# Transformer block on one core: three more matrix sections in seven products, two of the block sums added by DMA, one more raw buffer

## The chip, the cores and the metric

The kernel runs on one core of one Trainium2 chip. The metric is device microseconds of one execution, the median of several; lower is better. The engines are TensorE (PE; weight loads are listed as PEld), VectorE (DVE), ScalarE (ACT), GpSimd (POOL) and SyncE (SP), which here only issues DMAs. GpSimd can issue DMAs too.

## The reference

One layer of a hybrid block on x of 256 rows by 1024 columns, float32: a feed-forward with half weight, a token mixer, a second feed-forward. All projections take 1024 columns in; the feed-forwards go to 4096 and back.

```python
x = x + 0.5 * rmsnorm(swiglu(rmsnorm(x, pre1), w_gate, w_up, w_down), post1)
h = rmsnorm(x, mix_pre)
q, k, v, f, u, sv, ga, gb = split(h @ w_in)                  # 1024 each, f: 8
o_a = forgetting_attention(q, k, v, f)                       # 8 heads of 128, causal
o_b = gelu(u) * (w_s @ layernorm(gelu(sv)) + b_s)            # in groups of 128 columns
x = x + rmsnorm((sigmoid(ga) * o_a + sigmoid(gb) * o_b) @ w_out, mix_post)
x = x + 0.5 * rmsnorm(swiglu(rmsnorm(x, pre2), w_gate2, w_up2, w_down2), post2)
# swiglu(h, g, u, d) = (silu(h @ g) * (h @ u)) @ d
```

## The kernel before, in words

**Precision.** Every float32 operand is split into a high part (ScalarE, a cast, line 86) and a low part (VectorE, the difference, line 87), and every product is three matmuls: high by high, high by low, low by high. A weight quarter is 128 x 2048 floats, 1 MB: four blocks of 128 rows by 512 columns. It is loaded by SP into one of five `raws` buffers, split into a pair of `hi` and `lo` in one of four `wts` pairs, and then used by TensorE. A pair is free again when its last matmul has ended, and a raw buffer when both parts (and sums from it) are made.

**Sections.** A projection of 1024 by 1024 columns is a "section". The ordinary form (`section`, `section_by_tile`, line 223) takes the four quarters in turn and each serves both row tiles: 8 steps of 12 matmuls of 512 columns. The form in seven products (`fast`, line 298) is a Winograd scheme on 2 x 2 blocks: the activations in quarters, of which four sums (`parts`) are made once by `sums`, and the weights in quarters b11, b12, b22, b21, of which sums are made on the way. Each of seven products P1 to P7 is again 12 matmuls, with a split of its own for its weight (a quarter or a sum of quarters), and VectorE mixes the results (`u2`, `w`, `y11`, `y01`, `y10`, line 306). The weight sums are adds in the raw buffers (line 302). Before, this form is used for `up` of blocks 1 to 3 of both feed-forwards.

**Feed-forward.** `ffn` goes through four blocks of 1024 hidden columns: gate, then up, then the gated result is transposed (`hp`, `hT`). Between the steps of block b stand the down steps (`y`, line 363) of block b - 1, two groups of 12 matmuls from each down quarter (`d`). Block 0 has none, the last block's come at the end.

**Mixer.** v, then attention head by head, each with two half-heads of 16 matmul pairs; scores, transposes and values are put off by a few steps (`later`). Then sv with its LayerNorm, u, ga, gb and the output projection.

**Order.** Each engine runs its own instructions in the order of the program, which the scheduler of the building layer fixes; a wait holds up all that stands behind it on that engine. SP's loads are one queue; a load waits for its raw buffer. Norm gains are loaded into two buffers of their own (`gains`).

The lines that choose the form and hold the sums:

```python
FAST1 = {(b, "u") for b in range(1, NB)}
FAST2 = {(b, "u") for b in range(1, NB)}
FASTM = set()
...
    raws = ctx.enter_context(tc.tile_pool(name="raws", bufs=5))
    wts = ctx.enter_context(tc.tile_pool(name="wts", bufs=4))
    gains = ctx.enter_context(tc.tile_pool(name="gains", bufs=2))
```

## Time and profile before

| what | value |
|---|---|
| median of 3 runs | 751.82 us (751.54 to 752.13) |
| the profiled execution | 752.29 us, of which the span of the trace is 750.5 |
| granted TensorE clock over the span | 0.993 |
| busy: TensorE, VectorE, ScalarE, GpSimd | 736.4, 544.4, 380.0, 12.9 us |
| loaded from memory | 140.02 MB, 188 GB/s over the span |

The span runs from the first to the last instruction of the trace; the rest of the profiled execution lies around it. A share of busy time is a mean over stages that differ; what bounds a stage is read in its own window.

### The profile page before, as it was taken

How to read it: one execution, taken by the hardware profiler on the slowest of the kernel's cores; microseconds unless marked ns; L12 is line 12 of the kernel's file. 1: busy time of each engine (PE TensorE's matmuls, PEld its weight loads, DVE VectorE, ACT ScalarE, POOL GpSimd, SP SyncE). 2: the span in 40 equal slices, each digit the busy share in tenths (PEclk: the TensorE clock that was granted, in tenths of full speed). 3: DMA queues.
4: the chain of work that ended last, by engine and by line, in shares of the span. 5: the costliest groups of instructions: out<-in, count | busy, mean ns of one | idle time of the engine just before them, and what ended most of it. 6: DMA issues, size and time to landing. Idle time of an engine off the chain costs nothing.

```text
span 750.5 us, 8526 instructions
## 1 busy us (share of the span) xinstructions
PE 736.4 (98%) x3446; PEld 609.0 (81%) x3446; DVE 544.4 (73%) x565; ACT 380.0 (51%) x397; POOL 12.9 (2%) x20
## 2 busy tenths in 40 slices
...
GB/s 333 335 258 231 57 225 298 149 72 342 203 57 196 336 144 187 279 169 113 161 120 281 163 117 224 145 179 265 169 56 250 307 116 104 340 172 57 224 56 57
DMA packets 22695, 141.62 MB, mean 189 GB/s; under 512 B 3264, under 2 KB 3520, under 8 KB 6528
## 3 DMA queue, kind: packets, MB, share of 16 engines
q1 hardware_dynamic: 22656, 141.08, 51.4%
...
HBM read 140.02 MB, written 1.05 MB: 188 GB/s over the span
## 4 chain that ended last, share of the span: by engine, by line
PE 91%; DVE 4%; issue 1%; POOL 1%; ACT 1%; DMA 1%; SPq 0%; POOLq 0%; DVEq 0%; ACTq 0%
PE g L223 22%; PE y L363 22%; PE u L223 9%; PE qk L202 4%; PE sv L223 3%; PE ga L223 3%; PE gb L223 3%; PE qk L203 2%; PE hp L384 2%; PE v L223 2%; PE u_3D L298 1%; PE u_1C L298 1%; PE u_2C L298 1%; PE wo L223 1%; PE u_1D L298 1%; PE u_2D L298 1%
## 5 line engine op out<-in xcount | busy, mean ns | idle before, releaser
L223 PE MATMUL g<-hi_g,xT 128*128 128x512 f32 x512 | 165.8, 395 | 0.5 <-ACT xT L86 0.5
L363 PE MATMUL y<-hi_d,hT 128*128 128x512 f32 x512 | 147.4, 391 | 0.0
L223 PEld LDWEIGHTS g<-hi_g,xT 128*128 128x128 f32 x512 | 97.3, 190 | 21.3 <-ACT xT L86 1.3
L363 PEld LDWEIGHTS y<-hi_d,hT 128*128 128x128 f32 x512 | 95.7, 188 | 19.4
L87 DVE TENSOR_TENSOR lo_g<-raw_g,hi_g 128x2048 fp32r<-128x2048 f32 (+1 forms) x50 | 74.9, 1518 | 42.0 <-ACT hi_g L86 42.0
L223 PE MATMUL g<-lo_g,xT 128*128 128x512 f32 x256 | 100.7, 393 | 1.1 <-DVE lo_g L87 1.1
L87 DVE TENSOR_TENSOR lo_d<-raw_d,hi_d 128x2048 fp32r<-128x2048 f32 x32 | 73.0, 2286 | 36.8 <-ACT hi_d L86 36.6
L363 PE MATMUL y<-lo_d,hT 128*128 128x512 f32 x256 | 80.8, 392 | 0.0
L86 ACT CAST hi_g<-raw_g 128x2048 fp32r<-128x2048 f32 (+1 forms) x50 | 62.8, 1292 | 32.9 <-PE u L223 9.3
L86 ACT CAST hi_d<-raw_d 128x2048 fp32r<-128x2048 f32 x32 | 60.8, 1914 | 25.4 <-PE g L223 8.6
L223 PE MATMUL u<-hi_u,xT 128*128 128x512 f32 x192 | 60.6, 391 | 0.0
L223 PEld LDWEIGHTS g<-lo_g,xT 128*128 128x128 f32 x256 | 48.5, 190 | 11.9 <-DVE lo_g L87 2.1
L363 PEld LDWEIGHTS y<-lo_d,hT 128*128 128x128 f32 x256 | 47.8, 188 | 9.7
L302 DVE TENSOR_TENSOR raw_u<-raw_u,raw_u 128x2048 f32<-128x2048 f32 x24 | 55.0, 2292 | 0.8
L369 ACT ACTIVATE sg<-g 128x512 f32<-128x512 f32 x32 | 18.8, 597 | 60.5 <-PE g L223 60.5
L202 PE MATMUL qk<-xT,hi_qk 128*128 128x512 f32 x128 | 46.6, 405 | 0.0
L86 ACT CAST hi_u_3p<-raw_u 128x2048 fp32r<-128x2048 f32 x14 | 26.6, 1914 | 32.9 <-DVE raw_u L302 26.0
L223 PEld LDWEIGHTS u<-hi_u,xT 128*128 128x128 f32 x192 | 36.1, 188 | 7.3
L87 DVE TENSOR_TENSOR lo_u_3p<-raw_u,hi_u_3p 128x2048 fp32r<-128x2048 f32 x14 | 31.9, 2288 | 9.4 <-ACT hi_u_3p L86 9.4
L223 PE MATMUL u<-lo_u,xT 128*128 128x512 f32 x96 | 37.4, 389 | 0.0
L86 ACT CAST hi_u_2p<-raw_u 128x2048 fp32r<-128x2048 f32 x14 | 26.8, 1917 | 20.1 <-DVE raw_u L302 9.5
L86 ACT CAST hi_u_1p<-raw_u 128x2048 fp32r<-128x2048 f32 x14 | 26.8, 1917 | 20.1 <-DVE raw_u L302 9.5
(256 smaller groups left out, 1264.7 us busy)
## 6 DMA issues: line engine op xcount, KB each, us to landing
raw_u<-in_u SPq DMA_DIRECT2D x32, 1024.0 KB, 4.8
raw_d<-in_dn SPq DMA_DIRECT2D x32, 1024.0 KB, 4.8
raw_g<-in_g SPq DMA_DIRECT2D x30, 1024.0 KB, 4.9
raw_qk<-in_w_qk SPq DMA_DIRECT2D x8, 1024.0 KB, 5.0
raw_v<-in_w_v SPq DMA_DIRECT2D x4, 1024.0 KB, 5.2
raw_sv<-in_w_sv SPq DMA_DIRECT2D x4, 1024.0 KB, 4.8
raw_u<-in_w_u SPq DMA_DIRECT2D x4, 1024.0 KB, 4.7
raw_ga<-in_w_ga SPq DMA_DIRECT2D x4, 1024.0 KB, 4.8
```

The lines of the kernel that those rows point to most:

```text
L86: return [nc.scalar.copy(out=hi, in_=src), nc.vector.tensor_tensor(out=lo, in0=src, in1=hi.bitcast(F32), op=ALU.subtract)]
L87: nc.vector.tensor_tensor(out=lo, in0=src, in1=hi.bitcast(F32), op=ALU.subtract)]
L202: nc.tensor.matmul(ps, lhsT=hi, rhs=xT[:, k], start=k == 0, stop=False, skip_group_check=True)
L203: nc.tensor.matmul(top, lhsT=lo, rhs=xT[:, k, :, 0, :], start=False, stop=k == KT - 1, skip_group_check=True)
L223: nc.tensor.matmul(ps, lhsT=xT[:, kh * 4 + k, t, xs, :], rhs=v, start=kh == 0 and k == 0 and q == 0, stop=kh == 1 and k == 3 and q == 2)
L298: nc.tensor.matmul(ps, lhsT=lhs(k, xs), rhs=z, start=start and k == 0 and q == 0, stop=k == 3 and q == 2, skip_group_check=True)
L302: nc.vector.tensor_tensor(out=out, in0=p, in1=q, op=ALU.add)
L363: nc.tensor.matmul(ys[t][c], lhsT=hTs[f // 4][:, f % 4, t, xs, :], rhs=w[:, c * 512:(c + 1) * 512], start=f == 0 and q == 0, stop=f == NF ...
L369: nc.scalar.activation(out=sg, in_=y, func=AF.Silu)
L384: nc.tensor.transpose(out=ps[:, i * P:(i + 1) * P], in_=h[:, i * P:(i + 1) * P], identity=ident)
```

## The change

**Where seven products are used.** In both feed-forwards gate of block 2 joins the three ups, and in the mixer ga. The sums of activations for the mixer (`sums("mx")`) are made during attention, ahead of head 5, and ga is moved from behind u to the place right behind attention.

**Two sums by DMA.** Where gate of a block is in the set (block 2), and for ga, `fast` gets `dma=True`. The weight sums for P5 and P7 are then not adds of VectorE: one quarter is loaded by SP, and GpSimd issues a DMA that reads the second quarter and adds it to the buffer (`accum_op`). b12 is loaded twice. The sums for P6 and P4 stay with VectorE, so each such section has two sums on each side, where the section before had four on VectorE.

**Order of products.** P1 P5 P6 P2 P3 P7 P4 in place of P1 P5 P6 P2 P7 P3 P4, in all such sections; the sum for P4 is made right behind P2.

**Buffers.** Six raw buffers in place of five; the two gain buffers are gone, and gains are loaded as pairs into a raw buffer where they are used.

```diff
-FAST1 = {(b, "u") for b in range(1, NB)}
-FAST2 = {(b, "u") for b in range(1, NB)}
-FASTM = set()
+FAST1 = {(b, "u") for b in range(1, NB)} | {(2, "g")}
+FAST2 = FAST1
+FASTM = {"ga"}
...
-    raws = ctx.enter_context(tc.tile_pool(name="raws", bufs=5))
+    raws = ctx.enter_context(tc.tile_pool(name="raws", bufs=6))
-    gains = ctx.enter_context(tc.tile_pool(name="gains", bufs=2))
...
+    def gain(*names, by=D):
+        pair = raws.tile([P, 2048], F32, tag="raw", name=f"g_{names[0]}")
+        gs = [pair[:, i * D:(i + 1) * D] for i in range(len(names))]
...
-    def fast(src, name, parts, done):
+    def fast(src, name, parts, done, dma):
...
+        def two(first, second):
+            raw = get(*first)
+            nc.gpsimd.dma_start(out=raw, in_=src[second], accum_op=ALU.add)
+            return raw
...
-        b12 = get(1, 0)
-        add(b11, b11, b12)
+        if dma:
+            t1 = two((1, 0), (0, 0))
+        else:
+            b12 = get(1, 0)
+            add(b11, b11, b12)
+            t1 = b11
         c = bank(f"{name}C")
-        product(c, lhs_s(0), b11, "p5", True)
+        product(c, lhs_s(0), t1, "p5", True)
         yield
         b22 = get(1, 1)
-        add(b11, b11, b22)
+        add(b11, t1, b22)
...
-        add(b12, b12, b22)
         b21 = get(0, 1)
         product(a, lhs_x(1, 0), b21, "p2", False)
         done(0, 0, a)
+        add(b11, b11, b21)
         yield
-        d = bank(f"{name}D")
-        product(d, lhs_s(2), b12, "p7", True)
-        done(1, 1, mixed("y11", w, d, ALU.subtract))
-        yield
+        if not dma:
+            add(b12, b12, b22)
         product(c, lhs_s(3), b22, "p3", False)
         done(0, 1, mixed("y01", c, u2, ALU.subtract))
         yield
-        add(b11, b11, b21)
+        d = bank(f"{name}D")
+        product(d, lhs_s(2), two((1, 0), (1, 1)) if dma else b12, "p7", True)
+        done(1, 1, mixed("y11", w, d, ALU.subtract))
+        yield
         product(d, lhs_x(1, 1), b11, "p4", False)
...
-                    steps.append((fast(src, nm, parts, fn), 7))
+                    steps.append((fast(src, nm, parts, fn, (b, "g") in quick), 7))
...
-            later(1, lambda: values(pT))
+            later(1 if h < 6 else 2, lambda: values(pT))
...
-        parts = [sums("mx")] if FASTM else None
+        parts = []
...
-        oA = attention(v, *kept)
+        oA = attention(v, *kept, between=lambda: parts.append(sums("mx")))
+
+        def ga_done(t, c, ps):
+            oc = oA[:, t, c * 512:(c + 1) * 512]
+            sg = mid_tile([P, 512], f"sga{t}{c}")
+            nc.scalar.activation(out=sg, in_=ps, func=AF.Sigmoid)
+            later(5, lambda: nc.vector.tensor_tensor(out=oc, in0=oc, in1=sg, op=ALU.mult))
+
+        columns(a["w_ga"], "ga", ga_done)
```

The listings of the two programs count 3382 matmuls before and 3346 now; 599 instructions of VectorE in place of 561; five weight loads more on SP and ten DMAs on GpSimd.

**What this moves.** VectorE's order in the first feed-forward, from the low part (`lo`) of up's P4 in block 1 on. The names carry the section, block and product: `u1_1p4` is P4 of up, feed-forward 1, block 1, `g1_2` gate of block 2, `d1_8` a down quarter, `sg` a gating, `hT` the low part of a transposed half. Before:

```order
L87 TENSOR_TENSOR lo_u1_1p4_883<-raw_u1_100_693,hi_u1_1p4_882 128x2048
L306 TENSOR_TENSOR u1_1y11_825<-u1_1w_774,u1_1D_808 128x512
L87 TENSOR_TENSOR lo_g1_200_925<-raw_g1_200_922,hi_g1_200_924 128x2048
L376 TENSOR_TENSOR sg1_111_679<-u1_1y11_825,sg1_111_679 128x512
L87 TENSOR_TENSOR hT1_2_828<-hp1_100_829,hT1_2_828 128x4x128
L306 TENSOR_TENSOR u1_1y01_852<-u1_1C_717,u1_1u2_772 128x512
L87 TENSOR_TENSOR lo_d1_8_962<-raw_d1_8_959,hi_d1_8_961 128x2048
L376 TENSOR_TENSOR sg1_101_677<-u1_1y01_852,sg1_101_677 128x512
L87 TENSOR_TENSOR hT1_3_855<-hp1_111_856,hT1_3_855 128x4x128
L306 TENSOR_TENSOR u1_1y10_898<-u1_1D_808,u1_1u2_772 128x512
L376 TENSOR_TENSOR sg1_110_583<-u1_1y10_898,sg1_110_583 128x512
L87 TENSOR_TENSOR lo_g1_201_980<-raw_g1_201_977,hi_g1_201_979 128x2048
```

Now:

```order
L89 TENSOR_TENSOR lo_u1_1p4_880<-raw_u1_100_690,hi_u1_1p4_879 128x2048
L309 TENSOR_TENSOR u1_1y01_822<-u1_1C_714,u1_1u2_769 128x512
L89 TENSOR_TENSOR lo_g1_2p1_921<-raw_g1_200_917,hi_g1_2p1_920 128x2048
L390 TENSOR_TENSOR sg1_101_674<-u1_1y01_822,sg1_101_674 128x512
L89 TENSOR_TENSOR hT1_2_825<-hp1_100_826,hT1_2_825 128x4x128
L309 TENSOR_TENSOR u1_1y11_850<-u1_1w_771,u1_1D_833 128x512
L89 TENSOR_TENSOR lo_g1_2p5_950<-raw_g1_210_945,hi_g1_2p5_949 128x2048
L390 TENSOR_TENSOR sg1_111_676<-u1_1y11_850,sg1_111_676 128x512
L89 TENSOR_TENSOR hT1_3_853<-hp1_101_854,hT1_3_853 128x4x128
L309 TENSOR_TENSOR u1_1y10_895<-u1_1D_833,u1_1u2_769 128x512
L305 TENSOR_TENSOR raw_g1_200_917<-raw_g1_210_945,raw_g1_211_983 128x2048
```

The low part of P5 (its raw buffer `raw_g1_210` is the one that GpSimd adds to) stands where the low part of a down quarter stood, ahead of a gating, a transposed half, a mixed sum and the sum for P6.

Further on, VectorE's order in block 2, from the low part of up's P5 to that of P2. Before:

```order
L87 TENSOR_TENSOR lo_u1_2p5_1145<-raw_u1_200_1119,hi_u1_2p5_1144 128x2048
L302 TENSOR_TENSOR raw_u1_200_1119<-raw_u1_200_1119,raw_u1_211_1178 128x2048
L87 TENSOR_TENSOR lo_d1_12_1163<-raw_d1_12_1160,hi_d1_12_1162 128x2048
L87 TENSOR_TENSOR lo_u1_2p6_1183<-raw_u1_200_1119,hi_u1_2p6_1182 128x2048
L302 TENSOR_TENSOR raw_u1_200_1119<-raw_u1_200_1119,raw_u1_201_1203 128x2048
L87 TENSOR_TENSOR lo_u1_2p2_1206<-raw_u1_201_1203,hi_u1_2p2_1205 128x2048
```

Now:

```order
L89 TENSOR_TENSOR lo_u1_2p5_1160<-raw_u1_210_1155,hi_u1_2p5_1159 128x2048
L305 TENSOR_TENSOR raw_u1_200_1134<-raw_u1_210_1155,raw_u1_211_1193 128x2048
L309 TENSOR_TENSOR g1_2y10_1118<-g1_2D_1060,g1_2u2_1003 128x512
L89 TENSOR_TENSOR lo_d1_12_1178<-raw_d1_12_1175,hi_d1_12_1177 128x2048
L89 TENSOR_TENSOR lo_u1_2p6_1198<-raw_u1_200_1134,hi_u1_2p6_1197 128x2048
L305 TENSOR_TENSOR raw_u1_200_1134<-raw_u1_200_1134,raw_u1_201_1217 128x2048
L89 TENSOR_TENSOR lo_u1_2p2_1220<-raw_u1_201_1217,hi_u1_2p2_1219 128x2048
```

The last mixed sum of gate (`y10`) and the low part of `d12` now stand behind the low part of P5 and the sum that both read its buffer.

GpSimd's order up to the norms of the first feed-forward's end. Before:

```order
L154 TENSOR_TENSOR r_f10_120<-r_f10_120,power_91 128x1
L154 TENSOR_TENSOR r_f11_130<-r_f11_130,power_91 128x1
L154 TENSOR_TENSOR r_p10_1864<-r_p10_1864,power_91 128x1
L154 TENSOR_TENSOR r_mx0_1874<-r_mx0_1874,power_91 128x1
L154 TENSOR_TENSOR r_p11_1952<-r_p11_1952,power_91 128x1
L154 TENSOR_TENSOR r_mx1_1962<-r_mx1_1962,power_91 128x1
```

Now:

```order
L156 TENSOR_TENSOR r_f10_117<-r_f10_117,power_88 128x1
L156 TENSOR_TENSOR r_f11_127<-r_f11_127,power_88 128x1
L315 DMA raw_g1_210_945<-in_g1 128x2048
L315 DMA raw_g1_210_1061<-in_g1 128x2048
L315 DMA raw_u1_210_1155<-in_u1 128x2048
L315 DMA raw_u1_210_1277<-in_u1 128x2048
L156 TENSOR_TENSOR r_p10_1880<-r_p10_1880,power_88 128x1
L156 TENSOR_TENSOR r_mx0_1890<-r_mx0_1890,power_88 128x1
L156 TENSOR_TENSOR r_p11_1968<-r_p11_1968,power_88 128x1
```

Four adding DMAs of block 2 stand between the norms at the start and those at the end. In the mixer two stand ahead of the roots for sv's LayerNorm, and in the second feed-forward again four.

SP's order from the first load of block 2's gate. Before:

```order
L102 DMA raw_g1_200_922<-in_g1 128x2048
L102 DMA raw_d1_8_959<-in_dn1 128x2048
L102 DMA raw_g1_201_977<-in_g1 128x2048
L102 DMA raw_g1_210_1025<-in_g1 128x2048
L102 DMA raw_d1_10_1055<-in_dn1 128x2048
L102 DMA raw_g1_211_1073<-in_g1 128x2048
L102 DMA raw_u1_200_1119<-in_u1 128x2048
L102 DMA raw_u1_210_1140<-in_u1 128x2048
```

Now:

```order
L104 DMA raw_g1_200_917<-in_g1 128x2048
L104 DMA raw_g1_210_945<-in_g1 128x2048
L104 DMA raw_d1_8_965<-in_dn1 128x2048
L104 DMA raw_g1_211_983<-in_g1 128x2048
L104 DMA raw_g1_201_1007<-in_g1 128x2048
L104 DMA raw_g1_210_1061<-in_g1 128x2048
L104 DMA raw_d1_10_1084<-in_dn1 128x2048
L104 DMA raw_u1_200_1134<-in_u1 128x2048
L104 DMA raw_u1_210_1155<-in_u1 128x2048
L104 DMA raw_d1_12_1175<-in_dn1 128x2048
```

`raw_g1_210` and `raw_u1_210` each stand twice: first the load for P5's sum, then, behind b21 (`201`), the second load of b12 for P7's. The load for P5's sum takes the buffer that b21 of the section before has had.

## Rows read from the trace of the kernel before

**Rows 1.** The page's parts 1 and 3: busy times, DMA queue.

```profile
PE 736.4 (98%) x3446; PEld 609.0 (81%) x3446; DVE 544.4 (73%) x565; ACT 380.0 (51%) x397; POOL 12.9 (2%) x20
...
q1 hardware_dynamic: 22656, 141.08, 51.4%
```

**Rows 2.** The chain of waits in block 2: start, length, what.

```profile
133.24 5.44 PE g L223 x24
...
160.44 2.72 PE u_2C L298 x12
163.16 2.72 PE y L363 x12
...
168.60 2.72 PE u_2A L298 x12
```

**Rows 3.** Busy time by window, block 2 and its up half.

```profile
core 0: us, PE busy (x) PEld busy (x) DVE busy (x) ACT busy (x) POOL busy (x), PEclk, DMA share, GB/s
124.60:189.10 64.50, 64.50 (x293) 53.28 (x293) 50.91 (x33) 33.51 (x24) 0.00 (x0) 1.00 0.53 197
157.70:189.10 31.40, 31.40 (x146) 25.89 (x145) 30.20 (x22) 19.27 (x13) 0.00 (x0) 1.00 0.73 267
```

**Rows 4.** Timeline of VectorE: start, length, line, operation.

```profile
117.16 0.68 DVE L87 TENSOR_TENSOR hT<-hp,hT 128x512 fp32r<-128x512 f32 x1
117.76 0.68 DVE L306 TENSOR_TENSOR u_1y<-u_1C,u_1u 128x512 f32<-128x512 f32 x1
118.36 2.28 DVE L87 TENSOR_TENSOR lo_d<-raw_d,hi_d 128x2048 fp32r<-128x2048 f32 x1
120.55 0.68 DVE L376 TENSOR_TENSOR sg<-u_1y,sg 128x512 f32<-128x512 f32 x1
...
121.76 0.68 DVE L306 TENSOR_TENSOR u_1y<-u_1D,u_1u 128x512 f32<-128x512 f32 x1
...
145.72 4.62 DVE L302 TENSOR_TENSOR raw_u<-raw_u,raw_u 128x2048 f32<-128x2048 f32 x2
150.25 2.28 DVE L87 TENSOR_TENSOR lo_u_2p<-raw_u,hi_u_2p 128x2048 fp32r<-128x2048 f32 x1
```

**Rows 5.** Busy time by window: late attention, sv (columns as in rows 3).

```profile
330.00:360.00 30.00, 30.00 (x195) 27.07 (x194) 16.76 (x31) 14.78 (x33) 0.00 (x0) 1.00 0.40 136
360.70:386.70 26.00, 26.00 (x132) 21.84 (x132) 18.43 (x52) 12.35 (x20) 2.10 (x2) 1.00 0.27 86
```

**Rows 6.** Timeline of VectorE: the same step of two heads.

```profile
344.84 0.29 DVE L527 TENSOR_REDUCE nmx<-S 128x1 f32<-128x128 f32 x1 [2.64 <-PE S L522]
...
352.44 0.29 DVE L527 TENSOR_REDUCE nmx<-S 128x1 f32<-128x128 f32 x1 [2.64 <-PE S L522]
```

**Rows 7.** DMA issues: count, KB each, median us from issue to landing.

```profile
raw_u<-in_u SPq DMA_DIRECT2D x32, 1024.0 KB, 4.8
...
g_ffn_post_g<-in_ffn_post_g SPq DMA_DIRECT2D x2, 512.0 KB, 5.5
```

**Rows 8.** The view of one tile, gate's raw buffers: landings.

```profile
DMA to landing us min/median/max: 4.7/5.4/9.0
```

**Rows 9.** Timeline of SP's queue in block 1's up.

```profile
102.08 0.33 SPq L102 DMA_DIRECT2D raw_g<-in_g  x1
```

**Rows 10.** Timeline of ScalarE: casts, idle before them and what ended it.

```profile
115.53 1.92 ACT L86 CAST hi_d<-raw_d 128x2048 fp32r<-128x2048 f32 x1 [0.82 <-PE u_1C L298]
...
121.44 1.91 ACT L86 CAST hi_g<-raw_g 128x2048 fp32r<-128x2048 f32 x1 [2.84 <-PE u_1D L298]
...
124.62 1.91 ACT L86 CAST hi_g<-raw_g 128x2048 fp32r<-128x2048 f32 x1 [0.80 <-PE y L363]
```

More of the change, by code (lines that the diff above doesn't have):

```diff
@@ L76, in block @@
     nc.vector.memset(power, -0.5)
-    def gain(name, by=D):
-        g = gains.tile([P, D], F32, tag="g", name=f"g_{name}")
-        for c in range(0, D, by):
-            nc.sync.dma_start(out=g[:, c:c + by], in_=a[name][:, c:c + by])
-        return g
+    def gain(*names, by=D):
+        pair = raws.tile([P, 2048], F32, tag="raw", name=f"g_{names[0]}")
+        gs = [pair[:, i * D:(i + 1) * D] for i in range(len(names))]
+        for name, g in zip(names, gs):
+            for c in range(0, D, by):
+                nc.sync.dma_start(out=g[:, c:c + by], in_=a[name][:, c:c + by])
+        return gs
     def split(hi, lo, src):
@@ L493, in forget_gates, with attention @@
         nc.vector.tensor_copy(out=cs[:, 2], in_=cs[:, 0].bitcast(F32))
-    def attention(v, cs, idr, pick):
+    def attention(v, cs, idr, pick, between):
         oA = big.tile([P, NT, D], F32, tag="b", name="oA")
         for h in range(H):
+            if h == 5:
+                between()
             w = quarter(a["w_qk"][h // 2, h % 2], f"qk{h}")
@@ L561, in mixer @@
         run(section_by_tile(a["w_v"], "v", v_done, 4))
-        parts = [sums("mx")] if FASTM else None
+        parts = []
         def columns(src, name, done):
-            run(fast(src, name, parts, done) if name in FASTM else section(src, name, done))
-        oA = attention(v, *kept)
+            run(fast(src, name, parts, done, True) if name in FASTM else section(src, name, done))
+        oA = attention(v, *kept, between=lambda: parts.append(sums("mx")))
[5 more added lines that the diff above has]
+        columns(a["w_ga"], "ga", ga_done)
         ws = aux.tile([P, H, P], F32, tag="aux", name="ws")
@@ L575, in mixer @@
         nc.sync.dma_start(out=bs, in_=a["b_s"])
-        lng, lnb = gain("sgu_ln_g"), gain("sgu_ln_b")
+        lng, lnb = gain("sgu_ln_g", "sgu_ln_b")
         vn = big.tile([P, NT, D], F32, tag="b", name="vn")
@@ L617, in mixer @@
         columns(a["w_u"], "u", u_done)
-        def ga_done(t, c, ps):
-            oc = oA[:, t, c * 512:(c + 1) * 512]
-            sg = mid_tile([P, 512], f"sga{t}{c}")
-            nc.scalar.activation(out=sg, in_=ps, func=AF.Sigmoid)
-            nc.vector.tensor_tensor(out=oc, in0=oc, in1=sg, op=ALU.mult)
-        columns(a["w_ga"], "ga", ga_done)
         ms = {}
@@ L642, in mixer @@
         run(section_by_tile(a["w_gb"], "gb", gb_done))
-        gp, gn = gain("mix_post_g"), gain("ffn2_pre_g")
+        gp, gn = gain("mix_post_g", "ffn2_pre_g")
         ys, turn = {}, {}
```

10 lines of the change are left out of this document (6 added, 4 removed).

## The prediction

> **What bounds the kernel now.** I read the page's busy times first. TensorE is busy for 736.4 of 750.5 us, VectorE for 544.4, ScalarE for 380.0, and the DMA engines for 51.4% of the span [rows 1]. Only work taken from TensorE, or a new wait of TensorE, can move the time much. The chain of waits agrees: through the block that the change rebuilds it runs on TensorE alone, and every twelve 512-column matmuls take 2.72 us, whether they are a product of seven or a pair of down steps [rows 2].
>
> Then I looked at who is next. In block 2 of the first feed-forward (124.60 to 189.10 us) TensorE is busy for all 64.50 us, VectorE for 50.91, ScalarE for 33.51. In its up half alone VectorE already has 30.20 of 31.40 us, and the DMA engines 73% [rows 3]. The reader is to see that TensorE has the whole time, but its nearest follower has little left where products of seven run.
>
> **What is removed.** Each section in seven products has one product less: 12 matmuls, 2.72 us [rows 2]. Three sections change (gate of block 2 twice, ga once). The listing of TensorE's order has 36 matmuls fewer and no others more. So TensorE's work falls by 3 x 2.72 = 8.16 us.
>
> **What VectorE gets.** From start to start a 128x2048 low part costs 2.20 us (118.36 to 120.55), a 128x512 step 0.60 (117.16 to 117.76), two sums in SBUF 4.53 together (145.72 to 150.25), about 2.3 each [rows 4]. Block 2 gets three low parts and five mixed sums more; its SBUF sums stay four, since each half now leaves two to DMA. That is 3 x 2.20 + 5 x 0.60 = 9.6 us, so 60.5 us of VectorE beside 64.50 - 2.72 = 61.8 us of TensorE: 98%. No stall follows from this alone, but the lead that VectorE builds up no longer grows, and a late input is not caught up quickly.
>
> In ga VectorE has seven low parts, two sums, five mixed sums and four gatings, 7 x 2.20 + 2 x 2.3 + 9 x 0.60 = 25.4 us; three low parts and one sum (8.9) come before ga starts, during attention. From ga's start to the end of sv VectorE then has 25.4 - 8.9 + 18.43 (what the same sv stretch holds now) = 34.9 us, and TensorE 7 x 2.72 + 26.00 = 45.0 [rows 5]. That covers ga. The twelve 128x512 steps of the sums for the mixer, 12 x 0.60 = 7.2 us, go into attention, where a head takes 7.60 us (344.84 to 352.44) and VectorE is busy for 16.76 of 30.00 [rows 5, 6]; they are caught up within three heads. The first user behind them, the scores of head 5, comes three half-heads (11.4 us) after its inputs are asked for. I cost both at nothing; without the cover the sums alone would cost up to 7.2 us. ScalarE gets three casts of 1.92 and some copies per place and has 31 us free in the block.
>
> **The gains** now pass through the raw buffers and hold one of six while in use, so five are left there, as before. Each pair is queued ahead of the loads for v, sv and wo. Cover: a 512 KB gain and a 1 MB raw load both land in about 5 us [rows 7] and the pieces are asked for many microseconds ahead. Nothing. The new order of products moves P7 behind P3 and adds no work.
>
> **The sums by DMA** are the open price. Per seven-product section SP loads one weight block more (5 MB in all), and GpSimd adds a second block to a loaded one twice (10 sums in all). Nothing of GpSimd's own is queued behind them that is near: its next instructions are the roots of the norms at the end of the feed-forward, and in the mixer those of sv. What does wait is VectorE: the low part of P5 stands in its order ahead of mixed sums, down parts and the sum for P6, all of which are held up.
>
> I walk the first such place by the rows of VectorE, SP and ScalarE [rows 4, 9, 10], in the new order. VectorE reaches the low part of gate's P5 at 118.4. Its source gets its buffer when b21 of the up section is done with, where SP now issues a load at 102.08 [rows 9]; a load lands after 4.8 [rows 7], so at 106.9, and the sum is then issued. Call X the time from there until it has landed. From the sum's landing the path to P6's low part is cast 1.92 [rows 10], low part 2.20, five steps of 0.60 (two gatings, two transposed halves, a mixed sum), the sum for P6 2.3, d's low part 2.20, P6's own 2.28: 13.9 us. TensorE wants P6 at 133.2, where its matmuls go on behind the first down step now [rows 2]. So gate stalls by X - 12.4 if that is positive.
>
> The second place is tighter. VectorE goes on from y10 at 121.76: 0.60, sum for P6 2.3, two of 0.60, low part of d 2.20, of P6 2.20, one of 0.60, P2's 2.20, the sum for P4 2.3, and is at about 135.4; the weight buffers that ScalarE's casts wait for (released by the products' ends, as at 121.44 and 124.62 [rows 10]) are free in time. Only then is b21's buffer free for up's P5: load until 140.2, sum until 140.2 + X. Then: cast 1.92, low part 2.20, sum 2.3, mixed 0.60, d12 2.20, P6 2.20, sum 2.3, P2 2.28, 16.0 us in all. TensorE wants P2 at 168.60 - 2.72 = 165.9 [rows 2]. Up stalls by X - 9.7 if positive. The sums for P7 have 5 us more room each.
>
> X is in no row. From below: a plain load of the same size takes 4.7 us at least [rows 8], so no stall. From above: the sum reads the weights and the buffer it adds to, two passes, each at the slowest landing in a crowd, 9.0: 18 us [rows 8], stalls of 5.6 and 8.3, 27.8 us over both feed-forwards. I take two passes at the median of raw_g, where loads overlap, 2 x 5.4 = 10.8, nearest because up's sum runs beside four other loads (d12, u11, u01, the second u10) at a place where the DMA engines have 73% now. That gives 1.1 us in each up and none in gate; ga's two sums are loaded during attention, with 20 us or more of room.
>
> The Trainium skill, "DMA: Bandwidth & Descriptors", section "Anatomy of one DMA", gives a DMA from GpSimd about 2.0 us plus bytes over 436 GB/s; for 1 MB that is an estimate of 4.4 us, and the sum would have no stall. No run here shows it yet.
>
> **The sum.** The profiled execution took 752.28 us (span 750.5 and 1.8 around it): 752.3 - 8.2 + 2 x 1.1 = 746.3. The median of the runs is 751.82, 0.5 lower, so **745.8 us**, 0.8% faster. Within 0.2% (750.3 to 753.3) is what a measurement of this kernel can't tell from no change.
>
> **Rivals.** First, the sums are hidden altogether (X below 9.7): 751.8 - 8.2 = 743.7. For it: a lone load lands in 4.8, and two passes at that would be 9.6. Against it: the DMA engines' share, and 98% of VectorE. The figure of the Trainium skill's DMA page named above would end here.
>
> Second, the gain is mostly given back: X of 12 to 13.3 costs 2.3 to 3.6 in up and up to 0.9 in gate, twice: 4.6 to 9 us, 748.2 to 752.6. For it: four loads that each land alone in 4.8 fall into the same stretch as up's sum.
>
> Third, on the other side, slow sums: from X = 13 each further microsecond costs four (two places, two feed-forwards), the gain is gone at X = 13.1, and at 18 the time is 771. For it: no row shows a DMA from GpSimd, nor one that adds. Against it: ordinary loads of that size never take over 9.0. The Trainium skill, "SBUF — State Buffer", in its box on VectorE blocking DMA, says that GpSimd can't write descriptors while a VectorE instruction in a two-port mode holds the port they share; this speaks for slow sums, if VectorE's steps here were of that kind, which no row shows.
>
> Fourth, a wait outside the sums: VectorE's sums in attention, or ga and the LayerNorm of sv behind each other, stall TensorE for 4 to 8 us: 748 to 752. Against it: 34.9 of 45.0 us.
>
> **How the numbers follow.** Forecast (X about 9.7 to 12, 743.7 to 748.2): 0.40. Hidden: 0.28. Given back: 0.12. Slow: 0.14. Elsewhere: 0.06. The predicted time is the likeliest's. Hidden, forecast and the faster half of given back and elsewhere are faster by over 0.2%: 0.74. Same: 0.11. Slower: 0.15. The range reaches from 743.2 (no stall, less half a microsecond) to 751.5, which leaves out the slow sums and little else.
>
> **What would show it.** TensorE with 36 matmuls less and a busy time near 728; in block 2 one mark of the forecast is a wait of TensorE of about 1 us before up's P2 or d12, ended by VectorE, and before it a wait of ScalarE's cast of up's P5 that a DMA on GpSimd's queue ends. Landings of those sums near 11 us would show X right, under 9 the first rival, over 13 the third. VectorE at 97% or more in block 2 shows that part. In ga and sv no wait of TensorE over 1 us. The prediction is wrong if TensorE waits more than 5 us in block 2, or anywhere else for more than 2.

## The result and the profile after

The changed kernel takes **760.08 us** (median of 4 runs, 759.18 to 760.62) where the kernel before, run beside it, took 751.68 (751.32 to 752.13): ratio 1.0109, 95% interval 1.0097 to 1.0122. It is slower; 745.8 with a range of 743.2 to 751.5 was predicted, so the prediction was wrong, and on the wrong side. One of the four runs of p7_plain below took 1231 us at a granted clock of 0.56; the time given for it is the median of the other three.

First the page of the changed kernel, its busy times and DMA queues, beside [rows 1]:

```profile
PE 732.9 (97%) x3410; PEld 602.5 (79%) x3410; DVE 583.1 (77%) x603; ACT 401.8 (53%) x414; POOL 21.9 (3%) x30
...
q1 hardware_dynamic: 23376, 146.32, 51.6%
q0 software_dynamic: 1440, 10.49, 7.5%
```

TensorE has the 36 matmuls less, but its busy time fell by 3.5 us only, where 8.2 were forecast, and its idle time rose from 750.5 - 736.4 = 14.1 to 758.8 - 732.9 = 25.9. The new queue q0 holds the ten sums by DMA. Their landings, from the view of the DMA issues (count, KB each, median us from issue to landing), beside the plain loads:

```profile
raw_u<-in_u SPq DMA_DIRECT2D x34, 1024.0 KB, 5.0
...
raw_g<-in_g POOLq DMA_DIRECT2D x4, 1024.0 KB, 9.7
raw_u<-in_u POOLq DMA_DIRECT2D x4, 1024.0 KB, 11.2
...
raw_ga<-in_w_ga POOLq DMA_DIRECT2D x2, 1024.0 KB, 8.4
```

These medians mix the sums for P5, for which VectorE idles, with those for P7, which took 8.7 to 10.0 us in the feed-forwards. The four sums for P5 one by one, gate and up of the first feed-forward, then gate and up of the second:

```profile
DMA to landing us min/median/max: 11.6/11.6/11.6
...
DMA to landing us min/median/max: 12.7/12.7/12.7
...
DMA to landing us min/median/max: 9.5/9.5/9.5
...
DMA to landing us min/median/max: 12.8/12.8/12.8
```

So X, the disputed price, is near what was taken (10.8) by the medians, but 2 us above it for both of up's sums. The view of TensorE's waits (total, times, longest), of which the kernel before has neither the first, the second, the third nor the last:

```profile
PE hp L398 <- DVE sg L390: 4.0, 4, 2.4
...
PE y L377 <- DVE lo_d L89: 3.1, 2, 1.7
PE u_2A L301 <- DVE lo_u_2p L89: 3.0, 2, 1.5
...
PE u_3C L301 <- DVE u_3w L309: 0.7, 2, 0.3
```

All new waits are for VectorE. The largest is not in any product: `hp` are the transposes of the block before's gated values. Busy times by window, up of block 1 with the head of block 2's gate, the stretch behind it, and the rest of block 2 (columns as in [rows 3]):

```profile
93.60:124.62 31.02, 28.59 (x130) 23.25 (x128) 27.38 (x19) 18.67 (x12) 1.02 (x1) 1.00 0.72 237
124.62:131.00 6.38, 6.38 (x23) 5.17 (x24) 6.38 (x6) 2.23 (x2) 0.88 (x1) 0.73 0.68 116
131.00:195.50 64.50, 60.99 (x274) 49.23 (x273) 56.25 (x39) 37.66 (x28) 1.75 (x2) 1.00 0.86 295
```

TensorE idles 2.4 us ahead of 124.62, and then its granted clock is 0.73 over 6.38 us: a mean between its two levels of 1.2 and 2.4 GHz, which costs 6.38 x 0.27 = 1.7 us more. In the rest of block 2 it idles 3.5 us. The chain at the first place, read in four timelines (start, length; idle before and what ended it), GpSimd's, ScalarE's, VectorE's and TensorE's:

```profile
108.08 1.02 POOL L315 DMA_DIRECT2D raw_g<-in_g  x1 [98.21 <-DMA raw_g<-in_g]
...
145.01 0.88 POOL L315 DMA_DIRECT2D raw_u<-in_u  x1 [18.76 <-DMA raw_u<-in_u]
```

```profile
119.73 1.91 ACT L88 CAST hi_g_2p<-raw_g 128x2048 fp32r<-128x2048 f32 x1 [4.47 <-DMA raw_g<-in_g]
...
157.84 1.91 ACT L88 CAST hi_u_2p<-raw_u 128x2048 fp32r<-128x2048 f32 x1 [6.06 <-DMA raw_u<-in_u]
```

```profile
121.67 2.29 DVE L89 TENSOR_TENSOR lo_g_2p<-raw_g,hi_g_2p 128x2048 fp32r<-128x2048 f32 x1 [2.69 <-ACT hi_g_2p L88]
123.88 0.69 DVE L390 TENSOR_TENSOR sg<-u_1y,sg 128x512 f32<-128x512 f32 x1
...
159.78 2.29 DVE L89 TENSOR_TENSOR lo_u_2p<-raw_u,hi_u_2p 128x2048 fp32r<-128x2048 f32 x1 [5.73 <-ACT hi_u_2p L88]
...
171.90 4.49 DVE L89 TENSOR_TENSOR lo_u_2p<-raw_u,hi_u_2p 128x2048 fp32r<-128x2048 f32 x2
```

```profile
121.80 0.39 PE L301 MATMUL u_1D<-hi_u_1p,xT 128*128 128x512 f32 x1
124.62 0.65 PE L398 MATMUL hp<-ident,sg 128*128 128x128 f32 x4 [2.44 <-DVE sg L390]
```

The load of gate's P5 source has landed at 108.08 and its sum is issued; it lands at 119.7. ScalarE casts, VectorE has waited 2.69 us for that cast, and behind P5's low part in its order stands `sg`, the gating of up's y11. TensorE wants its transposes right behind P4's last matmul at 122. P5 itself is not needed before 132. At up of block 2 the sum is issued at 145.01, lands at 157.7, and VectorE idles 5.73 us; the low part of P2, the first of the two in the last row of VectorE, is done at 174.1.

In the second feed-forward gate's sum goes out as early, 14.3 us behind the start of its head (564.80; 14.5 in the first), but lands 2.1 us sooner, and the waits in the same rows are shorter:

```profile
579.10 0.92 POOL L315 DMA_DIRECT2D raw_g<-in_g  x1 [86.24 <-DMA raw_g<-in_g]
```

```profile
588.69 1.91 ACT L88 CAST hi_g_2p<-raw_g 128x2048 fp32r<-128x2048 f32 x1 [2.25 <-DMA raw_g<-in_g]
```

```profile
593.58 0.66 PE L398 MATMUL hp<-ident,sg 128*128 128x128 f32 x4 [0.24 <-DVE sg L390]
```

So f2's head loses little because the sum landed earlier; why it did is open.

Where the time went, by stages. Each number is the time from TensorE's first matmul of a stage to its first of the next, from its timeline; "f1" and "f2" are the feed-forwards, "head" goes from block 1's up to block 2's first product, "block 3" also holds the last down steps. The median and ratio to the kernel before are those of each kernel's own comparison.

| kernel | us | ratio (95%) | f1 head | f1 block 2 | f1 block 3 | mixer from ga/sv to wo | f2 head | f2 block 2 | f2 block 3 |
|---|---|---|---|---|---|---|---|---|---|
| before | 751.7 | | 31.3 | 64.5 | 87.7 | 95.9 | 31.4 | 64.5 | 87.0 |
| changed | 760.1 | 1.010-1.012 | 35.5 | 66.4 | 88.3 | 93.1 | 31.8 | 67.1 | 87.6 |
| no_sum | 745.3 | 0.989-0.992 | 31.4 | 61.9 | 88.3 | 93.1 | 31.4 | 61.9 | 87.5 |
| p5_plain | 745.5 | 0.991-0.993 | 31.4 | 61.8 | 88.3 | 93.1 | 31.4 | 61.8 | 87.5 |
| p7_plain | 760.9 | 1.011-1.014 | 35.9 | 67.8 | 88.3 | 93.1 | 32.0 | 66.7 | 87.5 |
| sum_behind | 746.7 | 0.992-0.995 | 31.4 | 62.8 | 88.3 | 93.1 | 31.4 | 62.4 | 87.5 |
| vector_sums | 762.2 | 1.012-1.015 | 31.4 | 68.8 | 88.3 | 95.6 | 31.4 | 68.8 | 87.6 |
| pinned | 762.0 | 1.012-1.015 | 31.4 | 69.6 | 88.4 | 93.1 | 31.4 | 69.4 | 87.6 |
| pinned_light | 760.3 | 1.009-1.013 | 33.0 | 67.9 | 88.4 | 93.1 | 31.4 | 68.0 | 87.6 |
| spare_vector | 756.6 | 1.005-1.008 | 35.8 | 62.6 | 88.2 | 94.9 | 31.9 | 63.8 | 87.5 |
| p2_second | 775.7 | 1.029-1.034 | 32.5 | 69.6 | 91.7 | 100.7 | 32.5 | 68.3 | 91.0 |
| old_order | 762.2 | 1.012-1.016 | 35.9 | 65.8 | 87.7 | 93.1 | 32.2 | 69.1 | 87.0 |
| ga_only | 749.5 | 0.996-0.998 | 31.4 | 64.5 | 88.3 | 93.1 | 31.4 | 64.5 | 87.5 |
| ga_old_order | 749.2 | 0.995-0.998 | 31.4 | 64.5 | 87.8 | 93.1 | 31.4 | 64.5 | 87.0 |
| ga_u | 756.2 | 1.005-1.008 | 31.3 | 64.5 | 88.3 | 99.6 | 31.4 | 64.5 | 87.5 |
| t1_first | 749.0 | 0.996-0.998 | 31.3 | 63.9 | 88.3 | 93.1 | 31.4 | 63.2 | 87.6 |
| **t1_early** | **745.4** | 0.991-0.994 | 31.4 | 61.9 | 88.3 | 93.1 | 31.4 | 61.8 | 87.5 |

In the changed kernel the mixer gives back 2.8 us, as forecast. Both blocks 2 should give 2.7 each; instead they, with their heads, take 4.2 + 1.9 + 0.4 + 2.6 us more, so 14.5 us are lost there. Block 3 loses 0.6 in each feed-forward.

### The profile page after: what moved, and what is told of

It is laid out like the page before. It is cut to its first block, busy times and chain, and to the rows that moved or that the text cites. A ratio compares the mean times of both kernels' runs of the same rounds, so it can differ in the third digit from the quotient of the medians.

```text
span 758.8 us, 8589 instructions
## 1 busy us (share of the span) xinstructions
PE 732.9 (97%) x3410; PEld 602.5 (79%) x3410; DVE 583.1 (77%) x603; ACT 401.8 (53%) x414; POOL 21.9 (3%) x30
## 4 chain that ended last, share of the span: by engine, by line
PE 46%; DVE 7%; DMA 4%; ACT 2%; issue 2%; POOL 0%; POOLq 0%; DVEq 0%; ACTq 0%
PE y L377 8%; PE g L225 7%; PE u L225 6%; PE qk L204 4%; PE gb L225 3%; PE sv L225 3%; PE qk L205 2%; DMA raw_g<-in_g 2%; DVE lo_u_2p L89 2%; PE v L225 2%; DMA raw_u<-in_u 2%; PE wo L225 1%; DVE lo_g L89 1%; PE hp L398 1%; PE gaA L301 1%
## 5 line engine op out<-in xcount | busy, mean ns | idle before, releaser
L225 PE MATMUL g<-hi_g,xT 128*128 128x512 f32 x384 | 124.7, 396 | 0.5 <-ACT xT L88 0.5
L89 DVE TENSOR_TENSOR lo_d<-raw_d,hi_d 128x2048 fp32r<-128x2048 f32 x32 | 73.2, 2286 | 26.1 <-ACT hi_d L88 25.9
L225 PEld LDWEIGHTS g<-hi_g,xT 128*128 128x128 f32 x384 | 73.2, 191 | 16.4 <-ACT xT L88 1.3
L89 DVE TENSOR_TENSOR lo_g<-raw_g,hi_g 128x512 fp32r<-128x512 f32 (+1 forms) x42 | 56.6, 1372 | 28.0 <-ACT hi_g L88 27.8
L225 PE MATMUL g<-lo_g,xT 128*128 128x512 f32 x192 | 75.8, 395 | 1.1 <-DVE lo_g L89 1.1
L88 ACT CAST hi_g<-raw_g 128x512 fp32r<-128x512 f32 (+1 forms) x42 | 47.5, 1174 | 23.6 <-PE u L225 9.6
L377 PEld LDWEIGHTS y<-lo_d,hT 128*128 128x128 f32 x256 | 47.9, 189 | 13.3 <-DVE lo_d L89 3.9
L305 DVE TENSOR_TENSOR raw_u<-raw_u,raw_u 128x2048 f32<-128x2048 f32 x20 | 45.8, 2290 | 0.5
L225 PEld LDWEIGHTS g<-lo_g,xT 128*128 128x128 f32 x192 | 36.6, 191 | 9.5 <-DVE lo_g L89 2.1
L89 DVE TENSOR_TENSOR lo_u_2p<-raw_u,hi_u_2p 128x2048 fp32r<-128x2048 f32 x14 | 31.9, 2287 | 12.9 <-ACT hi_u_2p L88 12.8
L88 ACT CAST hi_g_2p<-raw_g 128x2048 fp32r<-128x2048 f32 x14 | 26.8, 1916 | 21.4 <-PE g_2B L301 7.0
## 6 DMA issues: line engine op xcount, KB each, us to landing
raw_u<-in_u POOLq DMA_DIRECT2D x4, 1024.0 KB, 11.2
```

The lines of the kernel that those rows point to most:

```text
L88: return [nc.scalar.copy(out=hi, in_=src), nc.vector.tensor_tensor(out=lo, in0=src, in1=hi.bitcast(F32), op=ALU.subtract)]
L89: nc.vector.tensor_tensor(out=lo, in0=src, in1=hi.bitcast(F32), op=ALU.subtract)]
L225: nc.tensor.matmul(ps, lhsT=xT[:, kh * 4 + k, t, xs, :], rhs=v, start=kh == 0 and k == 0 and q == 0, stop=kh == 1 and k == 3 and q == 2)
L305: nc.vector.tensor_tensor(out=out, in0=p, in1=q, op=ALU.add)
L377: nc.tensor.matmul(ys[t][c], lhsT=hTs[f // 4][:, f % 4, t, xs, :], rhs=w[:, c * 512:(c + 1) * 512], start=f == 0 and q == 0, stop=f == NF ...
```

## The experiments

The first theory was that the sum is late at a bad place: VectorE meets P5's low part ahead of gatings that TensorE needs first.

**no_sum** drops the accumulating DMAs and keeps everything else.

```diff
-            nc.gpsimd.dma_start(out=raw, in_=src[second], accum_op=ALU.add)
```

> Leaves out part of the work: the accumulating DMA is dropped, so P5 and P7 of the sections with sums by DMA multiply the plain quarter instead of the sum; all matmuls, all work of VectorE and ScalarE and the order of every engine but GpSimd stay. Theory (late sums: the low part of P5 stands in VectorE's order ahead of the last gating of the block before, and waits there for the sum's landing): the stalls of block 2 go, 16.5 us lost less the order's 2 in block 3, so 744 to 748. Rival A (VectorE is simply full in block 2, 98% of the stretch, whatever the sums do): 757 or more. Rival B (the 10.5 MB more of traffic slow every load): also 744 to 748, so the next kernel must tell it from the theory.

Measured: 745.26 us, inside 744 to 748. No new wait is left in the blocks 2. VectorE's work is all there, in the head and in block 2:

```profile
93.60:125.00 31.40, 31.40 (x145) 25.90 (x144) 30.46 (x21) 19.28 (x13) 0.00 (x0) 1.00 0.54 201
125.00:186.90 61.90, 61.90 (x282) 50.96 (x281) 59.49 (x42) 39.76 (x28) 0.00 (x0) 1.00 0.72 270
```

VectorE is at 59.49 of 61.90 us, 96%, and TensorE does not wait for it once. Being full costs nothing by itself. Over both windows VectorE has 93.30 - 89.95 = 3.4 us idle; in the changed kernel, by the three windows above, 101.9 - 90.0 = 11.9. The stretch grew by 8.6 us and VectorE's idle time by 8.5; as its work is the same, that is one finding and not two.

**p2_second** makes P2 the second product, so that P5's low part stands behind the gatings.

```diff
+        b21 = get(0, 1)
+        product(a, lhs_x(1, 0), b21, "p2", False)
+        done(0, 0, a)
+        yield
         c = bank(f"{name}C")
         product(c, lhs_s(0), t1, "p5", True)
...
         w = mixed("w", c, u2, ALU.subtract)
-        yield
-        b21 = get(0, 1)
-        product(a, lhs_x(1, 0), b21, "p2", False)
-        done(0, 0, a)
         add(b11, b11, b21)
```

> The order of products becomes P1 P2 P5 P6 P3 P7 P4, with the same loads, the same sums by DMA and the same work. In VectorE's order the low part of P5 then stands behind the last gating and the last two transposed copies of the block before, and P5 itself is needed some 6 us later. Theory (late sums ahead of the gating): most of the 9.1 us lost around block 2 of the first feed-forward and of the 5.7 us in the second come back, 745 to 750. Rival A (VectorE is full) and rival B (traffic): no change from the changed kernel, 757 to 761.

Measured: 775.67 us. The head loses 1.2 us in place of 4.2, but all else gets worse, blocks 3 and ga too. In every section of seven products b21's buffer is now held past P6, until the sum for P4 is made; that this is the reason was not tried. In the waits of TensorE the down steps come first, and behind them one of attention's at 4.3 us that the kernel before hasn't:

```profile
PE y L377 <- DVE lo_d L89: 10.0, 4, 3.3
PE O L562 <- ACT pT L557: 4.3, 1, 4.3
```

It changed too much at once to decide between the theories.

**ga_only** takes gate of block 2 back to eight products, and the sums by DMA of block 2 with it.

```diff
-FAST1 = {(b, "u") for b in range(1, NB)} | {(2, "g")}
+FAST1 = {(b, "u") for b in range(1, NB)}
```

> The gate of block 2 goes back to eight products in both feed-forwards, and its and up's sums by DMA with it; ga in seven products with sums by DMA, six buffers and the new order of products stay. Theory: no late sum is left ahead of a gating; ga+sv gives back 2.7 us as measured in the changed kernel, and the new order costs up to 1, so 749.0 to 750.0. Rival C (the new order of products itself costs, 0.8 to 1.2 us as seen in block 3 of each feed-forward, and more in blocks 1 and 2): 751 to 754.

Measured: 749.50 us. The mixer's gain is real and sums by DMA cost nothing in ga; block 3's 0.6 us stays in both feed-forwards.

**vector_sums** keeps the three sections in seven products and makes all sums on VectorE.

```diff
-                    steps.append((fast(src, nm, parts, fn, (b, "g") in quick), 7))
+                    steps.append((fast(src, nm, parts, fn, False), 7))
...
-            run(fast(src, name, parts, done, True) if name in FASTM else section(src, name, done))
+            run(fast(src, name, parts, done, False) if name in FASTM else section(src, name, done))
```

> The same three sections in seven products, but all their sums on VectorE and none by DMA. Four sums of about 2.2 us more per block 2: VectorE would need 69 us in block 2 beside 61.8 of TensorE. Theory: no late sum, but now VectorE is the bound there by 7.5 us in each feed-forward: 743.6 + 15 + up to 2 = 757 to 761. A rival by which VectorE's load can spread over the neighbouring blocks gives 746 to 750.

Measured: 762.20 us, a little past the upper end. Block 2 takes 68.8 us where 61.8 + 7.5 = 69.3 was worked out: with all sums on VectorE more than the product saved is lost. In its window VectorE is busy for 64.81 us, less than the 69 expected, and idle for 4.0, in two waits of 2.0 us for casts of ScalarE, so the figure was met in part by luck:

```profile
123.50:192.30 68.80, 64.15 (x282) 50.66 (x281) 64.81 (x44) 38.20 (x28) 0.00 (x0) 1.00 0.50 184
```

**pinned** queues P5's split on both engines, and the add for P6, behind the last gating and transposed copy of the section before (gate), or its last mixed sum and activation (up).

```diff
-            w = parts_of(raw, f"{name}{nm}")
+            with ExitStack() as stack:
+                for i in behind:
+                    stack.enter_context(tc.issue_after(i))
+                w = parts_of(raw, f"{name}{nm}")
...
+            for z in behind if dma else ():
+                stack.enter_context(tc.issue_after(recent[z]))
+            add(b11, t1, b22)
```

> The changed kernel with one thing different: the split of P5's sum (ScalarE's high part, VectorE's low part) and VectorE's add for P6, in the gate and up sections of block 2, are queued behind the last gating and transposed copies of the section before. Loads, sums by DMA, products, traffic and VectorE's work stay. Theory (the late sum is waited for at the head of VectorE's and ScalarE's queues, ahead of work that TensorE needs first): TensorE no longer waits at the head of gate of block 2, and most of the 14.8 us lost around block 2 comes back: 745 to 750. Rival B (the sums' traffic slows the loads, wherever VectorE waits): 757 to 761, with the waits now at P5, P6 or P2 themselves. In between (750 to 757): both have a share.

Measured: 761.99 us; the first theory falls in this form. The head is whole again (31.4), and block 2 loses 7.7 us in place of 4.5. TensorE's waits now name P5 itself:

```profile
PE g_2C L306 <- ACT hi_g_2p L88: 5.0, 2, 2.5
...
PE u_2C L306 <- DVE lo_u_2p L89: 3.1, 2, 1.7
```

But ScalarE's part had been queued behind its copy of P1's result, too far, so a lighter one follows below.

**old_order** puts P7 ahead of P3 again and makes the sum for P4 last; **ga_old_order** does the same to ga_only.

```diff
-        add(b11, b11, b21)
...
+        d = bank(f"{name}D")
+        product(d, lhs_s(2), two((1, 0), (1, 1)) if dma else b12, "p7", True)
+        done(1, 1, mixed("y11", w, d, ALU.subtract))
+        yield
         product(c, lhs_s(3), b22, "p3", False)
         done(0, 1, mixed("y01", c, u2, ALU.subtract))
         yield
-        d = bank(f"{name}D")
...
+        add(b11, b11, b21)
```

> The changed kernel with P7 ahead of P3 again and the sum for P4 made last. Theory: the late sums of P5 stay where they are, so nearly the whole loss stays; block 3's 0.6 us in each feed-forward comes back, and P7's sum has 5 us less room: 758 to 764. If the order of products were what cost, it would give 745 to 752.

> Only ga in seven products (sums by DMA) and six buffers, with P7 ahead of P3 as in the kernel before. The stage table of the run with ga alone shows 0.6 us more in block 3 of each feed-forward than before; if that is the new order (w waits behind the sum for P4 on VectorE), this kernel gives 748.0 to 748.8, 1.1 below the run with ga alone. If it is something else (six buffers, other loads' times), 749.3 to 749.8.

Measured: 762.16 and 749.24 us. Blocks 3 are back at 87.7 and 87.0: the new order costs 0.5 to 0.6 us in each, where P3 waits for `w` with no P7 between. In all it is 0.3 us by the medians of ga_only and ga_old_order, whose runs overlap, and 1.0 by the stages; 749.24 lies in neither of the two ranges given for it. The order is not what made the kernel slow.

**ga_u** is ga_only with u in seven products too.

```diff
-FASTM = {"ga"}
+FASTM = {"ga", "u"}
```

> As the run with ga alone, and the mixer's u in seven products with sums by DMA as well. Theory (sums by DMA cost nothing where no gating waits behind them): another 2.7 us less, 746.5 to 747.5. If late sums cost wherever they are used, 749 to 755.

Measured: 756.24 us, a miss. One wait of TensorE is new, at 421 us, behind sv's LayerNorm. VectorE has 19.20 of 21.00 us there, and TensorE's granted clock is 0.84:

```profile
PE uA L301 <- DVE lo_up L89: 5.9, 1, 5.9
```

```profile
404.00:425.00 21.00, 15.07 (x63) 11.92 (x62) 19.20 (x50) 7.20 (x6) 2.75 (x3) 0.84 0.48 137
```

The sum for u's P5 had landed at 396.3, well before. VectorE's own work fills this place; the run says nothing on late sums.

**p5_plain** and **p7_plain** drop the accumulating DMA of one of the two (p5_plain's line; p7_plain does the same to P7's).

```diff
-            t1 = two((1, 0), (0, 0))
+            t1 = get(1, 0)
```

> Leaves out part of the work: P5 of the sections with sums by DMA (gate and up of block 2, ga) multiplies a plain quarter, without its accumulating DMA; P7's sums by DMA stay. Theory (the landing of P5's sum, some 10 us behind its load, stands in the path of VectorE, which has about 3 us to spare in the 93 us of up of block 1 and block 2): nearly all of the loss goes, 745 to 749. If P7's sums or the traffic of the sums share the loss evenly: 750 to 755.

> Leaves out part of the work: P7 of the same sections multiplies a plain quarter, without its accumulating DMA; P5's sums by DMA stay. Theory: the loss stays but for what P7's sums add by occupying the DMA while P5's of up are under way, 755 to 760. If P7's sums are the cost: 745 to 750.

Measured: 745.52 and 760.93 us. P5's sum carries the whole loss, P7's nothing that shows.

**sum_behind** issues as many sums, but behind the readers of the buffer, so that no engine waits for one.

```diff
-            t1 = two((1, 0), (0, 0))
+            t1 = get(1, 0)
...
         add(b11, t1, b22)
+        if dma:
+            nc.gpsimd.dma_start(out=t1, in_=src[0, 0], accum_op=ALU.add)
...
-        product(d, lhs_s(2), two((1, 0), (1, 1)) if dma else b12, "p7", True)
+        t7 = get(1, 0) if dma else b12
+        product(d, lhs_s(2), t7, "p7", True)
+        if dma:
+            nc.gpsimd.dma_start(out=t7, in_=src[1, 1], accum_op=ALU.add)
```

> Changes part of the computation: the same number of accumulating DMAs of the same size from the same tensors, but each is issued when the split and the sum for P6 have read its buffer, so that no engine waits for one; only a later load of the same buffer does. Theory (the time from load to landing is what costs, not the traffic): 745 to 750. Rival B (10.5 MB more of traffic, or buffers held some 10 us longer): 754 to 761.

Measured: 746.68 us. Traffic and the longer hold of the buffers cost 746.7 - 745.3 = 1.4 us here. The sums go out at other times than in the changed kernel, though (the first at 125.6 us, not 108.1), so traffic in the old places is excluded only with p7_plain, where half of it is gone and nothing comes back, and with t1_early below.

**t1_first** asks for P5's source, and its sum, ahead of P1's.

```diff
+        if dma:
+            t1 = two((1, 0), (0, 0))
         b11 = get(0, 0)
...
-        if dma:
-            t1 = two((1, 0), (0, 0))
-        else:
+        if not dma:
```

> The changed kernel with the load and sum for P5 issued ahead of the load for P1, one buffer earlier: in the changed kernel the two loads went out at 95.9 and 102.9 us for the gate, and the sum's load landed at 108; now the sum's load takes the first of the two. All sums by DMA stay. Theory: the sums for P5 land some 5 to 7 us earlier, VectorE's wait for them falls from 8.5 us over its share in the run without sums to 1 to 4 per feed-forward: 746 to 752. Rival B (traffic): 757 to 761 still.

Measured: 749.00 us, faster than before (interval 0.996 to 0.998). Gate's sum is issued at 100.27 instead of 108.08 and the head is whole; up's, issued at 135.77, lands 13.1 us later, and late in block 2 TensorE still waits 1.8 us for a gating:

```profile
100.27 1.02 POOL L315 DMA_DIRECT2D raw_g<-in_g  x1 [90.27 <-DMA raw_g<-in_g]
...
135.77 0.88 POOL L315 DMA_DIRECT2D raw_u<-in_u  x1 [12.50 <-DMA raw_u<-in_u]
```

```profile
PE hp L398 <- DVE sg L390: 2.9, 2, 1.8
```

**spare_vector** keeps the sums by DMA and takes one add per such section off VectorE.

```diff
-        add(b11, b11, b21)
+        if not dma:
+            add(b11, b11, b21)
```

> Leaves out part of the work: in the sections with sums by DMA, VectorE's add for P4's sum (2.29 us; two in each block 2, one in ga) is dropped; every sum by DMA stays as late as it is. If VectorE's lack of spare time is what turns the wait into loss: some 3 to 4.6 us come back in each feed-forward, 751 to 755. If only the place of the wait in its queue counts: at the head of gate of block 2 nothing changes, 758 to 761.

Measured: 756.59 us, between the two theories. At f1's head nothing comes back (35.8), and TensorE's wait for the gating is there as before:

```profile
PE hp L399 <- DVE sg L391: 3.8, 4, 2.7
```

Inside the blocks 2, 3.8 and 3.3 of the 4.5 and 5.2 us lost come back. But up's sum is not as late as it was: gate's dropped add was the last reader of the buffer that the source of up's P5 is loaded into. Counted from the first product of block 2 the sum landed after 23.4 us in place of 28.6 in f1, and after 28.3 in place of 29.3 in f2. Up's own dropped add, 2.2 us from start to start, stands between that landing and P2. In f2 these two, 1.0 and 2.2 us, make up the 3.3 that came back; so the run does not show what VectorE's spare time is worth in general. (1.8 us are lost in the mixer, where TensorE now waits 1.5 us for ga's w.)

**pinned_light** pins VectorE's part alone, behind the last gating (gate) or mixed sum (up).

```diff
-            w = parts_of(raw, f"{name}{nm}")
+            with ExitStack() as stack:
+                if behind:
+                    stack.enter_context(tc.issue_after(recent[behind]))
+                w = parts_of(raw, f"{name}{nm}")
```

> The changed kernel with only VectorE's low part of P5 and its add for P6 queued behind the last gating of the section before; ScalarE's high part of P5 stays where it was, ahead of TensorE's need. If the place in VectorE's queue is what costs: TensorE's wait for the gating (2.4 us) and what follows go, 747 to 753. If VectorE's idle time counts wherever it falls: 755 to 761, with the waits at other places.

Measured: 760.34 us. The head gets back 2.5 of its 4.2 us, and f1's block 2 loses 1.5 more. The wait moves, it doesn't go:

```profile
PE u_2C L306 <- DVE lo_u_2p L89: 3.7, 2, 1.8
...
PE y L385 <- ACT hi_d L88: 1.7, 4, 0.6
PE hp L406 <- DVE sg L398: 1.4, 1, 1.4
```

**t1_early** asks for P5's source and sum of both sections one product earlier still, in the section before.

```diff
+    def ahead(src, name):
+        ready[name] = load(src[1, 0], f"{name}10")
+        nc.gpsimd.dma_start(out=ready[name], in_=src[0, 0], accum_op=ALU.add)
...
-            t1 = two((1, 0), (0, 0))
+            t1 = ready.pop(name) if name in ready else two((1, 0), (0, 0))
...
+                    if (b, at) in ((1, 14), (2, 6)) and (2, "g") in quick:
+                        ahead(gs[2] if b == 1 else us[2], f"{'gu'[b - 1]}{n}_2")
                     tick()
```

> The changed kernel with the load and sum for P5 of both sections of block 2 issued one product earlier still, behind P7 of the section before and ahead of its load for P4 or down-projection. All sums stay by DMA. If the loss follows the time of landing: the remaining 3 to 4 us of the run with the sum's load first go too, 745 to 748. If loads that are moved back by it become late in their turn: 749 to 754.

Measured: **745.37 us**, ratio 0.9922 (0.9907 to 0.9936), with every sum still by DMA. It beats the kernel before and is as fast as no_sum. In f1 GpSimd issues the sums for P5 at 84.05 and 130.84, ScalarE's cast at 115.12 no longer waits for a DMA, and block 2 is as without sums, with the DMA engines at 92%. The issues:

```profile
84.05 1.02 POOL L289 DMA_DIRECT2D raw_g<-in_g  x1 [74.12 <-DMA raw_g<-in_g]
...
130.84 0.87 POOL L289 DMA_DIRECT2D raw_u<-in_u  x1 [9.96 <-DVE hT L89]
```

The sums also land sooner after their issue, these two in 7.9 and 8.3 us:

```profile
DMA to landing us min/median/max: 7.9/7.9/7.9
...
DMA to landing us min/median/max: 8.3/8.3/8.3
```

The first has no other load beside it, the second three; in the changed kernel four stood beside each of P5's sums in the feed-forwards. So the earlier request gained twice. The time of the second sum (VectorE is busy for all of it), ScalarE's cast, and block 2:

```profile
130.84:139.18 8.34, 8.34 (x38) 6.91 (x37) 8.34 (x5) 4.06 (x3) 0.87 (x1) 1.00 1.01 266
```

```profile
115.12 1.92 ACT L88 CAST hi_g_2p<-raw_g 128x2048 fp32r<-128x2048 f32 x1 [0.82 <-PE u_1D L307]
```

```profile
124.00:185.90 61.90, 61.90 (x282) 50.95 (x281) 59.52 (x42) 39.77 (x28) 1.74 (x2) 1.00 0.92 310
```

## Why the prediction was wrong

**What is removed** was right: 36 matmuls, and 2.6 to 2.8 us per section wherever nothing is late (no_sum's blocks 2 at 61.9 for the 61.8 worked out, and the mixer's 93.1 for 95.9). ga was right too. In the changed kernel ga and sv take 45.00 us, as predicted, without a wait:

```profile
367.50:412.50 45.00, 45.00 (x217) 37.63 (x216) 39.18 (x68) 29.49 (x33) 2.12 (x2) 1.00 0.60 212
```

VectorE has 39.18 us there instead of 34.9, without effect. The sums for the mixer, the gains and six buffers cost nothing that a stage shows.

**VectorE's work in block 2** was sized right (59.5 in no_sum against 60.5). X was right only as a median (8.4 to 11.2 us against 10.8), not for the sums that decide. The figure of the Trainium skill, "DMA: Bandwidth & Descriptors", section "Anatomy of one DMA", from which 4.4 us had been estimated, is too low here for a DMA that adds: a sum with no other load beside it took 7.9 us (t1_early), and with four 9.5 to 12.8, where the plain loads beside them, on SP's queue, took up to 11.7 in place of about 5. The box in "SBUF — State Buffer" is neither borne out nor refuted: GpSimd's DMA instructions take 0.9 to 1.0 us each, and a sum landed in 8.3 us with VectorE busy all the while, but no run separates a lock from the transfer.

**The step that failed** is "the path to P6's low part ... 13.9 us. TensorE wants P6 at 133.2 ... So gate stalls by X - 12.4". The path lists "two gatings, two transposed halves" as lengths only. Each has a need of its own, and the first comes long before P6: TensorE's transposes stand right behind P4, and wanted the gating at 122.2. By the prediction's own numbers the gating ends at 106.9 + 10.8 + 1.92 + 2.20 + 0.60 = 122.4, with nothing to spare. The sum then went out at 108.1, 1.2 us later than taken, and landed 11.6 after; cast, low part and gating ended near 124.6: a stall of 2.4 us where the formula has next to none. The clock, for which there was no term, took 1.7 more. f1's head lost 4.2 us. f2's, with the sum after 9.5 us, lost 0.4.

**The second step that failed** is the size of X in "Up stalls by X - 9.7". The walk itself was right: its first wait of TensorE is at d12 as marked, the path from the landing to P2's low part took 16.4 us (157.7 to 174.1) for the 16.0 worked out, and the sum went out 15.9 and 16.5 us behind the first product of block 2 (129.12 and 596.61), where 15.6 had been taken. But the sum took 12.7 and 12.8 us, not 10.8, which was the median of plain loads doubled. Of the 4.5 and 5.2 us that the blocks 2 lost, 1.1 each was forecast, 1.9 and 2.0 are X, 0.3 and 0.9 its later issue, 0.4 the path, and 0.7 a wait behind P2, for a gating of up, which again had no deadline in the working.

So neither the place in the queue alone (pinned, pinned_light) nor VectorE's fullness alone (no_sum) makes the loss. A sum that lands 9.5 to 12.8 us after its issue meets an engine with 3.4 us to spare, and the wait comes out at one place or another; if the sum is asked for earlier, there is none. The walk with the measured landings, the gatings and the clock put in accounts for nearly all that the heads and blocks 2 lost. Why sums of one size take 7.9 to 12.8 us was not tried: the loads beside them differ, but gate's sum, with the same four beside it, took 11.6 in f1 and 9.5 in f2.

**The new order "adds no work"** is true, but it adds a wait: 0.5 to 0.6 us in each block 3.

**The rivals.** The second had X right for up's sums (12 to 13.3) and gives 748.2 to 752.6; the measured time lies past it, since the gating, the clock and the new order's wait are not in it. By X alone 760 would need more than 15, which the landings don't show. The first rival's time, 743.7, is what a hidden sum is worth; t1_early reached 745.4, 1.1 of the difference being the new order. The rule given for a wrong prediction was met by the 2.44 us at f1's head, more than 2 outside block 2. In the rest of f1's block 2 TensorE waits 3.5, and VectorE is busy for 87% there, not for 97: its work is as forecast, but the stretch is longer.
